# One decoder step on one core: w_ada unsplit on TensorE in four column groups, identity products between its blocks, and DVE operations put at the end of a step

## The chip, the cores and the metric

The kernel runs on one core of a Trainium2 chip. Its engines are TensorE (PE in the rows; its weight loads are PEld), VectorE (DVE), ScalarE (ACT), GpSimd (POOL) and SyncE (SP), whose queue issues the transfers (DMA). The metric is the device time of one execution in microseconds, the median of several runs.

## The reference

One layer over a prompt of 2048 tokens and 8 sampled sequences of 4 tokens, model width 1024, all in float32. Two groups of heads stand side by side: HGRN2 (8 heads, a gated linear recurrence) and mLSTM (4 heads, a matrix memory).

```python
mod = jnp.dot(jax.nn.silu(c), w_ada) + b_ada            # c: one row for the prompt, 8 for the sampled sequences
shift, scale, gate = jnp.split(mod, 3, axis=-1)
h = _rms(x, norm_g) * (1 + scale[:, None]) + shift[:, None]
proj = jnp.dot(h, w_in) + b_in                           # q, f, i(v), z of HGRN2; u, z, o and two gates of mLSTM
o_h, S_new = _hgrn2(qh, logf, vh, S_h, chunk)            # chunkwise; exact per token
y_h = _head_rms(o_h, hgrn_norm_g) * silu(hz)
xc = silu(causal_conv4(mu)); q, k, v = block-diagonal products of xc, xc, mu
h_m, C, n, m = _mlstm(q, k, v, ig, logsigmoid(mf), C, n, m, chunk)
y_m = (_head_rms(sigmoid(mo) * h_m, mnorm_g) + skip * xc) * silu(mz)
out = x + gate[:, None] * jnp.dot(concat(y_h, y_m), w_out)   # then a last RMS norm
```

## The kernel before, in words

**Float32 in pieces.** A large product is made of float32r operands: a tensor is split into a rounded high part (a copy on ACT, line 206) and a low part (a difference on POOL or DVE, line 207), and three products (high-high, low-high, high-low) take the place of one.

**The start.** SyncE issues the loads in program order. `ada_rows` (lines 448 to 470) streams the first 2048 columns of w_ada, 8 MB, as 16 pieces of 128 x 1024, with four in flight. Each is split by ACT and by DVE (every fourth by POOL), and four products of 512 columns per piece, with 42 stationary columns `scs` (silu(c), high and low parts), add into four banks of PSUM. Between the pieces `ada_step` issues small loads and the norm of the first two x tiles. `ada_shift_scale` (lines 472 to 486) brings the rows out, transposes them and forms `msh` (shift) and `msc` ((1 + scale) times norm_g). Then the first unit of w_in is split (`stream_unit(0)`), and `x_modulate` transposes a scaled x tile, applies msc and msh into `hst` and splits the result into `hhi` and `hlo`, the stationary operands of every projection.

**The steady part.** The prompt is worked in four segments (`s`) of 512 tokens. In each segment 48 units of w_in columns follow in a written order (`ORDER`): wide units v and o (256 columns, `proj_tok`, line 563) and narrow units f, q, z, mu, mz (128 columns, `proj_ct`, line 549). In segment 0 units are loaded raw, split, and their parts stored in DRAM (`wdr`); later segments load the parts. A ring of four buffers (tag `w8`) holds the split weights, three buffers (tag `raw`) the raw ones.

**Steps.** After each group of products of a unit, `pump` lets every generator of the list `rec` issue its next piece of work: `hgrn` and `hgrn_out` of a head, `conv`, `mlstm`, `gates`, `bd_prep` (block-diagonal matrices from the small weights, `bd_fill`), statistics of the next x tiles. A generator's yields say how many steps later its next products come, so that TensorE finds them ready between the projection products. Engines work through their instructions in program order. In `hgrn` a chain of states goes from DVE (`U`, line 677) to POOL (`pscale`, line 121) and back, four times a head. `mlstm_out` scales `num` on POOL by a factor `fin` that DVE forms after four ACT squares; three steps later TensorE transposes it (`ph`, line 1324).

**The end.** The output product with w_out (line 1743), from about 1850 us on, is touched by nothing in the change.

## Time and profile before

| | |
|---|---|
| time, median of 3 runs | 2248.98 us (2247.84 to 2250.97) |
| the profiled execution: its own time | 2243.03 us |
| its span, first to last instruction | 2241.2 us |
| PE busy | 2170.0 us, 97% of the span |
| DVE, ACT, POOL busy | 57%, 44%, 19% |
| mean granted TensorE clock | 0.989 |
| transfers | 405.26 MB, mean 181 GB/s |

The busy shares are means over stages with different limits. A busy time of PE counts pipelined products whose ends are modelled, so in what follows the starts of instructions are read rather than their lengths. The granted clock is 1.00 at TensorE's upper level (2.4 GHz) and 0.50 at its lower one (1.2 GHz).

### The profile page before, as it was taken

To read this page: it belongs to the slowest core of one execution; us is meant where nothing else is said; L and a number is where in the kernel's file an instruction comes from. 1 tells how busy PE (TensorE), PEld (TensorE's weight loads), DVE (VectorE), ACT (ScalarE), POOL (GpSimd) and SP (SyncE) were. 2 spreads that over 40 slices of the span, in tenths; PEclk is the share of its full clock that TensorE was granted. 3 is DMA by queue.
4 is the path that set the end of the run, shared out by engine and by line. 5 is a ranking of instruction groups with operands and counts; after the bars stand their busy time and mean duration, and the time that the engine had idled before them with its cause. 6 is when DMAs were issued, how large, how long until landed. Compare 5 with 4: busy or idle time off the path is not lost.

```text
span 2241.2 us, 35168 instructions
## 1 busy us (share of the span) xinstructions
PE 2170.0 (97%) x13594; PEld 1915.1 (85%) x13594; DVE 1268.8 (57%) x2664; ACT 979.1 (44%) x2260; POOL 432.0 (19%) x436
## 2 busy tenths in 40 slices
PE   6999999999999999999999999999999998999998
PEld 3888998787899889899988898888899987888885
DVE  7675657566756574566574555655455675423232
ACT  6445554464443354353444454534444535212121
POOL 3424353341112020212010212110101033000000
PEclk8999999999999999999999999999999999999999
DMA  7676766864546465634465555454555566533330
GB/s 257 214 234 219 262 221 205 302 227 155 189 152 228 167 230 193 217 136 158 179 203 202 189 192 180 162 169 163 146 194 161 174 193 173 165 108 96 93 99 27
DMA packets 225318, 405.26 MB, mean 181 GB/s; under 512 B 24843, under 2 KB 168627, under 8 KB 196470
## 3 DMA queue, kind: packets, MB, share of 16 engines
q1 hardware_dynamic: 225142, 402.92, 54.2%
q8 instruction: 109, 1.79, 0.3%
q14 instruction: 67, 0.55, 0.1%
HBM read 298.43 MB, written 104.44 MB: 180 GB/s over the span
## 4 chain that ended last, share of the span: by engine, by line
PE 68%; DVE 4%; ACT 3%; DMA 1%; issue 1%; POOL 1%; SPq 0%; DVEq 0%; ACTq 0%; POOLq 0%
PE pct L549 27%; PE pout L1743 15%; PE ptok L563 11%; PE p L1151 1%; PE pc L1135 1%; PE pv L1064 1%; PE pp L663 1%; PE pa L639 1%; PE pq L1081 1%; PE po L687 1%; PE po L689 1%; PE psx L1108 1%; ACT st L92 1%; PE p L1135 1%; DMA raw<-in_w_out_dram 1%
## 5 line engine op out<-in xcount | busy, mean ns | idle before, releaser
L549 PE MATMUL pct<-hhi,w 128*128 128x512 f32 (+1 forms) x3200 | 852.0, 354 | 1.2 <-DVE S L697 1.2
L549 PEld LDWEIGHTS pct<-hhi,w 128*128 128x128 f32 x3200 | 552.9, 188 | 74.4 <-issue 3.3
L549 PE MATMUL pct<-hlo,w 128*128 128x512 f32 (+1 forms) x1600 | 560.6, 350 | 0.0
L549 PEld LDWEIGHTS pct<-hlo,w 128*128 128x128 f32 x1600 | 301.0, 188 | 39.2
L563 PE MATMUL ptok<-whi,hhi 128*128 128x256 f32 x1024 | 301.4, 294 | 4.4 <-ACT hhi L92 3.3
L563 PE MATMUL ptok<-whi,hlo 128*128 128x256 f32 x1024 | 291.2, 284 | 0.2 <-DVE hlo L426 0.2
L563 PE MATMUL ptok<-wlo,hhi 128*128 128x256 f32 x1024 | 290.9, 284 | 0.0
L1743 PE MATMUL pout<-wh,y 128*128 128x512 f32 (+1 forms) x792 | 247.2, 391 | 3.0 <-ACT wh L92 3.0
L563 PEld LDWEIGHTS ptok<-whi,hhi 128*128 128x128 f32 x1024 | 197.4, 193 | 7.8 <-ACT hhi L92 3.7
L563 PEld LDWEIGHTS ptok<-wlo,hhi 128*128 128x128 f32 x1024 | 197.6, 193 | 2.3 <-issue 2.2
L563 PEld LDWEIGHTS ptok<-whi,hlo 128*128 128x128 f32 x1024 | 197.3, 193 | 0.9 <-DVE hlo L426 0.9
L1743 PEld LDWEIGHTS pout<-wh,y 128*128 128x128 f32 (+1 forms) x792 | 148.2, 187 | 35.8 <-ACT wh L92 3.5
L1743 PE MATMUL pout<-wl,y 128*128 128x512 f32 (+1 forms) x408 | 159.8, 392 | 1.1 <-POOL wl L1780 0.6
L92 ACT ACTIVATE xo<-oo 128x512 f32<-128x512 f32 (+1 forms) x34 | 21.5, 632 | 249.5 <-DVE oo L1831 249.5
L92 ACT ACTIVATE e<-e 128x512 f32<-128x512 f32 (+1 forms) x160 | 102.0, 638 | 58.9 <-DVE e L1034 54.8
L1826 DVE TENSOR_TENSOR oo<-pout,gate 128x512 f32<-128x512 f32 x32 | 22.0, 687 | 186.3 <-PE pout L1743 185.4
L617 POOL TENSOR_SCALAR tn<-tn,noml,oml 128x512 f32<-128x512 f32 (+1 forms) x32 | 52.6, 1643 | 385.5 <-ACT G L92 384.8
L207 POOL TENSOR_TENSOR w<-raw,w 128x1024 fp32r<-128x1024 f32 x40 | 97.2, 2436 | 113.5 <-ACT w L92 95.1
L121 POOL TENSOR_SCALAR num<-num,fin 128x256 f32<-128x256 f32 x64 | 35.1, 566 | 401.7 <-DVE fin L1313 357.8
L1161 DVE SCALAR_TENSOR_TENSOR Cc<-Cc,dec,pc 128x258 f32<-128x258 f32 x120 | 52.4, 478 | 84.0 <-PE pc L1135 84.0
L1743 PEld LDWEIGHTS pout<-wl,y 128*128 128x128 f32 (+1 forms) x408 | 75.6, 185 | 19.7 <-POOL wl L1780 1.3
L1032 DVE SCALAR_TENSOR_TENSOR xc<-mu,cols,xc 128x512 f32<-128x512 f32 (+1 forms) x120 | 83.7, 698 | 4.2
(403 smaller groups left out, 3792.2 us busy)
## 6 DMA issues: line engine op xcount, KB each, us to landing
w<-wdr SPq DMA_DIRECT2D x120, 1024.0 KB
wdr<-w SPq DMA_DIRECT2D x40, 1024.0 KB
raw<-in_w_in_dram SPq DMA_DIRECT2D x56, 512.0 KB
whi<-wdr SPq DMA_DIRECT2D x24, 1024.0 KB
wlo<-wdr SPq DMA_DIRECT2D x24, 1024.0 KB
raw<-ydr SPq DMA_DIRECT2D x29, 512.0 KB
xt<-in_x_prompt_dram SPq DMA_DIRECT2D x28, 512.0 KB
raw<-in_w_ada_dram SPq DMA_DIRECT2D x16, 512.0 KB
```

The source lines that it names most:

```text
L92: nc.scalar.activation(out, in_, func, bias=bias, scale=scale, **kw)
L121: pool.tensor_scalar(out, in_, sc, 0.0, op0=ALU.mult, op1=ALU.add)
L207: eng.tensor_tensor(lo, raw, hi.bitcast(F32), op=ALU.subtract)
L549: pe.matmul(ps[:, :n], w[:, k, :], h[:, k, t0:t0 + n], start=(i == 0), stop=(i == 3 * KD - 1))
L563: pe.matmul(ps[:, :2 * P], h[:, k, t0:t0 + n], w[:, k, :], start=(i == 0), stop=(i == 3 * KD - 1))
L617: pool.tensor_scalar(tn[:, :W], tn[:, :W], noml[:, h:h + 1], oml[:, h:h + 1], op0=ALU.mult, op1=ALU.add)
L639: pe.matmul(pa[:, t], kt[:, t], qt[:, t])
L663: pe.matmul(pp[:, c * CH:c * CH + CH], ktT[:, c], v[:, c, vc])
L1032: vec.scalar_tensor_tensor(o, src(r), C("cw", 8 * r + k), o, op0=ALU.mult, op1=ALU.add)
L1135: pe.matmul(out[:, :DH + 2], a[:, x], b[y][:, c], start=(q == 0), stop=(q == 2))
L1161: vec.scalar_tensor_tensor(Cc[:, j], Cc[:, j], dec[:, i, c:c + 1], pcs[j][:, :DH + 2], op0=ALU.mult, op1=ALU.add)
L1743: pe.matmul(acc[g][:n if n == CH else 2 * n], a, b[:, 512 * g:512 * g + 512], start=(k == 0 and q == 0), stop=(k == KO - 1 and q == len(mm ...
```

## The change

- **w_ada.** `ada_rows` no longer splits. It loads eight blocks of 128 x 2048 (four in flight, in the ring's buffers) and multiplies them as float32: for each block four products of 512 columns with the same 32 stationary columns `sct` (9 used, the rest zero), each into its own group of 32 rows of one PSUM bank. `ada_shift_scale` becomes one copy, four transposes, two additions and the multiplication by norm_g. The high and low parts `scs` are still made, later (`gate_prep`), for the gate columns.
- **Identity products.** `fill` issues products of the identity with itself into an unread bank: 10 ahead of the first block, 5 behind each block, 3 behind the last, 10 ahead of the first modulation.
- **First unit.** Its first half is split by ACT and POOL, its second by ACT and DVE, with the DVE difference put between the modulation and the split of the first x tile.
- **`late`.** A list of operations that `pump` issues after all generators of the step have issued theirs. Into it go the scan and scaling operations of `hgrn`, the normalisation and the last products of `hgrn_out`, the last product of `conv`, the scaling of `num` and the last products of `mlstm_out`, with their stores.
- **Moved between engines.** The state scaling in `hgrn` goes from POOL to DVE; the fills of `bd_prep` from DVE to POOL.
- **Reordered.** In `mlstm` the splits of a chunk's head; the bias rows of a wide unit are loaded at the end of the wide unit before; the x tiles of the next segment are scaled on POOL a unit, or a step, later than they are loaded.

```diff
...
@@ -440,49 +446,43 @@
     def toks(smp):
         return [(c, c * CH, CH) for c in range(NCH)] + ([(NCH, SEG, NSM)] if smp else [])
-    NB = 1 + NSEQ
-
-    def ada_piece(n):
-        k, b = divmod(n, 2)
-        t = Bt("wada", [P, D]) if n % 2 else raw_tile()
-        sync.dma_start(t, w_ada[k * P:k * P + P, b * D:b * D + D])
+    def fill(junk, n):
+
+        for _ in range(n):
+            pe.matmul(junk[:, :P], ident, ident)
+
+    def ada_load(k):
+        t = ring.tile([P, 2 * D], F32, tag="w8", name="wada", bufs=4)
+        sync.dma_start(t, w_ada[k * P:k * P + P, :2 * D])
         return t
     def ada_rows(step):
-        acc = [ps_tile("pada") if b % 2 else ps_tile("pada") for b in range(4)]
-        raw = {n: ada_piece(n) for n in range(4)}
-        for n in range(2 * KD):
-            k, b = divmod(n, 2)
-            step(n)
-            r = raw.pop(n)
-            t = ring.tile([P, 2, D], F32R, tag="w8", name="wadas", bufs=4)
-            act(t[:, 0], r, AF.Copy)
-            (pool if n % 4 == 3 else vec).tensor_tensor(t[:, 1], r, t[:, 0].bitcast(F32), op=ALU.subtract)
-            for g in range(2):
-                c = slice(512 * g, 512 * g + 512)
-                for y in range(2):
-                    pe.matmul(acc[2 * b + g][:ML], scs[:, k], t[:, y, c], start=(k == 0 and y == 0),
-                              stop=(k == KD - 1 and y == 1))
-            if n + 4 < 2 * KD:
-                raw[n + 4] = ada_piece(n + 4)
+        junk, acc = ps_tile("fill"), ps_tile("pada")
+        fill(junk, 10)
+        w = {k: ada_load(k) for k in range(4)}
+        for k in range(KD):
+            step(k)
+            t = w.pop(k)
+            for q in range(4):
+                pe.matmul(acc[32 * q:32 * q + 32], sct[:, k], t[:, 512 * q:512 * q + 512], start=(k == 0),
+                          stop=(k == KD - 1), skip_group_check=True)
+            fill(junk, 5 if k < KD - 1 else 3)
+            if k + 4 < KD:
+                w[k + 4] = ada_load(k + 4)
         return acc
     def ada_shift_scale(acc):
-        rows = Bt("arows", [NB, D])
-        rows2 = Bt("arows", [NB, D])
-        for b in range(4):
-            dst = (rows, rows2)[b // 2][:, 512 * (b % 2):512 * (b % 2) + 512]
-            act(dst, acc[b][:NB], AF.Copy)
-            vec.tensor_tensor(dst, dst, acc[b][32:32 + NB], op=ALU.add)
-        for r, dst, one in ((rows, msh, 0.0), (rows2, msc, 1.0)):
-            ps = ps_tile("padt")
-            for k in range(KD):
-                pe.transpose(ps[:, k * NB:k * NB + NB], r[:, k * P:k * P + P], ident[:NB, :NB])
-            v = ps[:, :KD * NB].rearrange("p (k b) -> p k b", k=KD)
-            c0 = KD if one else 0
-            vec.scalar_tensor_tensor(dst, v, one, acol[:, c0:c0 + KD, None].to_broadcast([P, KD, NB]),
-                                     op0=ALU.add, op1=ALU.add)
+        r = Bt("arows", [P, 512])
+        vec.tensor_copy(r, acc)
+        ps = ps_tile("padt")
+        for c in range(4):
+            pe.transpose(ps[:, c * P:c * P + P], r[:, c * P:c * P + P], ident)
+        v = ps.rearrange("p (c q b) -> p q c b", c=4, q=4)
+        for x, dst in ((0, msh), (1, msc)):
+            vec.tensor_tensor(dst.rearrange("p (g c) b -> p g c b", g=2), v[:, 2 * x:2 * x + 2, :, :NB],
+                              acol[:, x * KD:x * KD + KD].rearrange("p (g c) -> p g c", g=2)[:, :, :, None]
+                              .to_broadcast([P, 2, 4, NB]), op=ALU.add)
         vec.tensor_tensor(msc, msc, C8("norm_g")[:, :, None].to_broadcast([P, KD, NB]), op=ALU.mult)
     def ada_gate(g, u):
...
@@ -584,6 +585,8 @@
             for g in list(rec):
                 if next(g, "end") == "end":
                     rec.remove(g)
+            while late:
+                late.popleft()()
     def drain(g=None):
         while rec and (g is None or g in rec):
@@ -609,12 +612,16 @@
         G = M("G")
         sigmoid(tn[:, :W], tn[:, :W])
         act(G[:, :W], tn[:, :W], AF.Ln, bias=lb[:, h:h + 1], scale=oml[:, h:h + 1])
-        vec.tensor_tensor_scan(G[:, :W], hmask[:, :W], G[:, :W], 0.0, op0=ALU.mult, op1=ALU.add)
         g4 = G[:, :SEG].rearrange("p (c u t) -> p c u t", u=2, t=CH // 2)
         mid = small("mid", [P, NCH, 1])
-        vec.tensor_copy(mid, g4[:, :, 0, CH // 2 - 1:CH // 2])
-        vec.tensor_tensor(g4[:, :, 0], g4[:, :, 0], mid.to_broadcast([P, NCH, CH // 2]), op=ALU.subtract)
-        pool.tensor_scalar(tn[:, :W], tn[:, :W], noml[:, h:h + 1], oml[:, h:h + 1], op0=ALU.mult, op1=ALU.add)
+
+        def decays():
+            vec.tensor_tensor_scan(G[:, :W], hmask[:, :W], G[:, :W], 0.0, op0=ALU.mult, op1=ALU.add)
+            vec.tensor_copy(mid, g4[:, :, 0, CH // 2 - 1:CH // 2])
+            vec.tensor_tensor(g4[:, :, 0], g4[:, :, 0], mid.to_broadcast([P, NCH, CH // 2]), op=ALU.subtract)
+            pool.tensor_scalar(tn[:, :W], tn[:, :W], noml[:, h:h + 1], oml[:, h:h + 1], op0=ALU.mult, op1=ALU.add)
+
+        late.append(decays)
         yield
         yield
         Ep = M("Ep")
@@ -626,9 +633,13 @@
             act(sm[:, 2 * NCH:], G[:, SEG:].rearrange("p (q t) -> p q t", t=SLEN)[:, :, SLEN - 1], AF.Exp)
         act(G[:, :W], G[:, :W], AF.Exp, scale=-1.0)
         beta = small("beta", [P, NCH])
-        vec.tensor_tensor(beta[:, :NCH - 1], sm[:, 0:NCH - 1], sm[:, NCH + 1:2 * NCH], op=ALU.mult)
-        vec.tensor_tensor(Ep[:, :W], hq[:, :W], Ep[:, :W], op=ALU.mult)
-        vec.tensor_tensor(tn[:, :W], tn[:, :W], G[:, :W], op=ALU.mult)
+
+        def scaled():
+            vec.tensor_tensor(beta[:, :NCH - 1], sm[:, 0:NCH - 1], sm[:, NCH + 1:2 * NCH], op=ALU.mult)
+            vec.tensor_tensor(Ep[:, :W], hq[:, :W], Ep[:, :W], op=ALU.mult)
+            vec.tensor_tensor(tn[:, :W], tn[:, :W], G[:, :W], op=ALU.mult)
+
+        late.append(scaled)
         kt, qt = tn, Ep
         yield
         yield
@@ -675,7 +686,7 @@
             else:
                 u = small("U", [P, P], 1)
                 vec.tensor_tensor(u, R[c], pc, op=ALU.add)
-                pscale(nxt, u, sc)
+                vec.tensor_scalar(nxt, u, sc, None, op0=ALU.mult)
             if c < NCH - 1:
                 R[c + 1] = nxt
         store(sdr[h] if s < NSEG - 1 else hgrn_p[0, 0, h], nxt)
...
@@ -1310,9 +1325,13 @@
                 act(junk[:n], nm[:n, c, :DH], AF.Square, scale=f[:n, 1, c:c + 1], accum=f[:n, 2, c:c + 1])
             act(ss, ss, AF.Ln, scale=1.0 / DH, bias=epsc[:n])
             act(ss, ss, AF.Exp, scale=-0.5)
-            vec.tensor_tensor(kap, ss, rh, op=ALU.mult)
-            for c in range(nch):
-                pscale(nm[:n, c, :DH], nm[:n, c, :DH], f[:n, 3, c:c + 1])
+
+            def scale(nm=nm, n=n, nch=nch, f=f):
+                vec.tensor_tensor(f[:n, 3, :nch], f[:n, 2, :nch], f[:n, 1, :nch], op=ALU.mult)
+                for c in range(nch):
+                    pscale(nm[:n, c, :DH], nm[:n, c, :DH], f[:n, 3, c:c + 1])
+
+            late.append(scale)
         yield
         yield
         yield
...
@@ -1367,10 +1390,16 @@
         units += us
     start.append(len(units))
-    def bias_bc(c0):
-        t = small("bb", [P, 2 * P], 1)
-        sync.dma_start(t, bcast_ap(b_in[0, c0:c0 + 2 * P], P))
-        return t
+    bias = {}
+
+    def bias_load(u):
+
+        while u < len(units) and units[u][1] not in ("v", "mo"):
+            u += 1
+        if u < len(units):
+            c0 = (OI if units[u][1] == "v" else OMO) + 2 * units[u][2] * P
+            bias[u] = small("bb", [P, 2 * P], 1)
+            sync.dma_start(bias[u], bcast_ap(b_in[0, c0:c0 + 2 * P], P))
     KO = 2 * D // P
     KA, NH = 4, 3
...
@@ -1542,7 +1573,7 @@
                 pe.matmul(ps[:, :P], bt[k - 2][:, 2], bt[k - 2][:, 3])
                 if k % 4 == 2:
                     bo = Bt("bo", [P, 4, 2, P])
-                bd_fill(bo[:, (k - 2) % 4, 0], 2, k - 2, vec)
+                bd_fill(bo[:, (k - 2) % 4, 0], 2, k - 2, pool)
                 vec.tensor_copy(bo[:, (k - 2) % 4, 1], ps[:, :P])
                 if k % 4 == 1:
                     store(bdd[:, k - 5:k - 1], bo)
...
@@ -1568,25 +1599,43 @@
         x_rstd(0, c)
         x_scale(0, c, x0[c][0], x0[c][2])
-    def ada_step(n):
-        if n < len(row_loads):
-            sync.dma_start(*row_loads[n])
-        if n in (1, 3):
-            x0.append(x_load(0, len(x0)))
-        if n in (6, 8):
-            x_norm(n // 2 - 3)
-        if n == 13:
+    pre = []
+
+    def ada_step(k):
+        if k < 4:
+            for d in row_loads[4 * k:4 * k + 4]:
+                sync.dma_start(*d)
+        if k == 0:
+            x0.append(x_load(0, 1))
+        if k in (2, 4):
+            x_norm(k // 2 - 1)
+        if k == 3:
+            gate_prep()
+        if k == 4:
+            pre.extend(x_transpose(x0[0][0], CH, g) for g in range(2))
+        if k == 5:
             cols_prep()
+    x0.append(x_load(0, 0))
     acc = ada_rows(ada_step)
-    assert len(row_loads) <= 13
+    assert len(row_loads) <= 16
     load_pieces(1)
     for c in range(2, NCH):
         x0.append(x_load(0, c))
-    pre = [x_transpose(x0[0][0], CH, g) for g in range(2)]
     ada_shift_scale(acc)
-    stream_unit(0)
-    x_modulate(*x0[0], pss=pre, eng=None)
+
+    class Lazy:
+        def tensor_tensor(self, *a, **k):
+            late.append(lambda: vec.tensor_tensor(*a, **k))
+
+    def flush():
+        while late:
+            late.popleft()()
+
+    stream(0)
+    stream(0, eng=Lazy())
+    fill(ps_tile("fill"), 10)
+    x_modulate(*x0[0], pss=pre, eng=None, mid=flush)
     x_norm(2)
     x_modulate(*x0[1], eng=None)
     x_norm(3)
...
@@ -1665,6 +1715,8 @@
         def x_next(c):
             nxt[c] = x_load(s + 1, c)
+
+        def x_now(c):
             x_scale(s + 1, c, nxt[c][0], nxt[c][2])
         def after_last(k_):
@@ -1672,12 +1724,17 @@
                 x_next(k_ + 2)
             if k_ < NCH:
                 x_modulate(*nxt.pop(k_))
+            if k_ + 2 < NCH:
+                x_now(k_ + 2)
         for j in range(per):
             u = base + j
             if j == per - 2 and not last:
                 x_next(0)
                 x_next(1)
+            if j == per - 1 and not last:
+                x_now(0)
+                x_now(1)
             if j == (5 if s == 0 else 1 if last else 2):
                 g = gates(s)
                 next(g)
...
```

## Rows read from the trace of the kernel before

**Rows 1.** The page's line of the span and, from its first section, the line of busy time (us, share of the span, instructions) of each engine.

```profile
span 2241.2 us, 35168 instructions
...
PE 2170.0 (97%) x13594; PEld 1915.1 (85%) x13594; DVE 1268.8 (57%) x2664; ACT 979.1 (44%) x2260; POOL 432.0 (19%) x436
```

**Rows 2.** What TensorE waited for, over the whole span: who waited <- for whom, us in total, times, the longest in us.

```profile
PE pada L465 <- DVE wadas L461: 7.9, 5, 3.4
PE ph L1324 <- POOL num L121: 6.7, 4, 4.2
PE po L689 <- DVE R L674: 4.2, 3, 3.2
PE pb L1542 <- DVE bt L1554: 4.2, 1, 4.2
...
PE pa L639 <- DVE tn L631: 3.6, 5, 1.1
...
PE pxt L397 <- POOL xt L121: 1.8, 1, 1.8
```

**Rows 3.** Busy time by stretches of the start: the stretch in us, its length, busy us and instructions of each engine, granted TensorE clock (1.00 is the upper level), busy share of the DMA engines, GB/s.

```profile
4.00:24.00 20.00, 10.53 (x33) 3.95 (x32) 14.74 (x28) 13.25 (x25) 7.26 (x4) 1.00 1.02 398
24.00:28.00 4.00, 2.98 (x7) 1.30 (x8) 3.57 (x3) 3.91 (x5) 1.34 (x2) 0.66 0.65 206
44.00:60.00 16.00, 13.85 (x88) 13.29 (x88) 10.50 (x26) 14.87 (x38) 9.20 (x5) 0.79 0.82 219
48.00:52.00 4.00, 4.00 (x21) 4.00 (x21) 2.60 (x7) 3.91 (x11) 1.12 (x1) 0.50 0.48 23
```

**Rows 4.** The start in order of time, all engines: start in us, duration in us, engine, line, operation, out<-in, partitions x elements, how many merged, and in brackets the idle time before and what ended it.

```profile
6.28 1.04 ACT L92 ACTIVATE wadas<-raw 128x1024 fp32r<-128x1024 f32 x1
...
32.30 3.28 DVE L461 TENSOR_TENSOR wadas<-wada,wadas 128x1024 fp32r<-128x1024 f32 x1
...
41.42 0.23 DVE L484 SCALAR_TENSOR_TENSOR msh<-padt,acol 128x72 f32<-128x72 f32 x1
41.54 4.65 POOL L207 TENSOR_TENSOR wlo<-raw,whi 128x1024 fp32r<-128x1024 f32 x2 [7.03 <-ACT whi L92]
...
42.16 1.82 DVE L486 TENSOR_TENSOR msc<-msc,cols 128x72 f32<-128x72 f32 x1
...
46.15 0.58 PE L563 MATMUL ptok<-whi,hhi 128*128 128x256 f32 x1 [3.27 <-ACT hhi L92]
...
63.50 0.63 PE L549 MATMUL pct<-hhi,w 128*128 128x512 f32 x2
```

**Rows 5.** TensorE in order of time, columns as in rows 4: two fp32 products of 512 columns (pq), eight of 257 columns into four groups of 32 output rows (p2S), four of 128 columns (pa) and four transposes (pk). An fp32 product leaves two records, a transpose one.

```profile
154.44 1.88 PE L1081 MATMUL pq<-xc,bm 128*128 128x512 f32 x4
...
156.27 0.28 PE L563 MATMUL ptok<-wlo,hhi 128*128 128x256 f32 x1
156.39 0.28 PE L563 MATMUL ptok<-whi,hlo 128*128 128x256 f32 x1
...
785.26 0.42 PE L1248 MATMUL p2S<-raw,qsS 128*32 128x257 f32 x3
...
785.94 0.39 PE L1248 MATMUL p2S<-raw,qsS 128*32 128x257 f32 x3
...
786.27 0.75 PE L1259 MATMUL pcS<-vs,kx 128*128 128x258 f32 x4
...
317.97 1.13 PE L639 MATMUL pa<-Ep,tn 128*128 128x128 f32 x8 [1.13 <-DVE tn L631]
318.94 0.60 PE L642 MATMUL pk<-ident,tn 128*128 128x128 f32 x4
```

**Rows 6.** The stretch of 100 to 130 us as in rows 3, one DVE operation from PSUM as in rows 4, and the block-diagonal fills on DVE and on POOL (line, engine, operation, count: shortest/median/longest ns, first and last start in us).

```profile
100.00:130.00 30.00, 24.80 (x124) 20.86 (x123) 27.28 (x58) 11.65 (x30) 11.10 (x8) 0.89 0.48 123
...
117.76 0.75 DVE L1441 TENSOR_SCALAR sz<-pct,cols 128x512 f32<-128x512 f32 x1
...
L331 DVE TENSOR_TENSOR bt<-bdw,oh x16: 277/282/1957, 73.1 to 154.6; 128x128 f32<-128x128 f32 x16
...
L331 POOL TENSOR_TENSOR bdf<-bdw,oh x8: 388/487/844, 1481.9 to 1840.2; 128x128 f32<-128x128 f32 x8
```

**Rows 7.** What DVE waited for, over the whole span, columns as in rows 2.

```profile
DVE fin L1313 <- ACT fin L92: 55.1, 20, 3.1
DVE U L677 <- POOL R L121: 48.7, 89, 2.6
...
DVE v L1486 <- DMA bb<-in_b_in_dram: 28.9, 9, 5.4
...
DVE hlo L426 <- POOL hhi L424: 17.9, 12, 8.9
```

**Rows 8.** The stretch of 500 to 510 us as in rows 3, and the POOL operation in it that scales an x tile, as in rows 4.

```profile
500.00:510.00 10.00, 8.15 (x57) 7.88 (x56) 2.90 (x7) 3.92 (x8) 3.31 (x4) 0.83 0.72 299
...
504.60 1.12 POOL L121 TENSOR_SCALAR xt<-xt,rstd 128x1024 f32<-128x1024 f32 x1 [16.62 <-DMA xt<-in_x_prompt_dram]
```

**Rows 9.** SyncE's queue waiting for DVE at the bias load, TensorE's weight loads waiting for num (both as in rows 2), and three terms of a convolution on DVE (as in rows 4).

```profile
SPq L1372 <- DVE mo L1486: 59.3, 8, 13.0
...
PEld ph L1324 <- POOL num L121: 9.5, 10, 4.7
...
1537.33 2.32 DVE L1032 SCALAR_TENSOR_TENSOR xc<-mu,cols,xc 128x512 f32<-128x512 f32 x3
```

More of the change, by code (lines that the diff above doesn't have):

```diff
@@ L234, in keep, with split @@
                     sync.dma_start(self.kept[i], x.bitcast(F32))
-        def split(self, j):
+        def split(self, j, eng):
             if self.again:
@@ L240, in split @@
             c = slice(P * j, P * j + P)
-            split(self.raw.pop(j), self.hi[:, :, c], self.lo[:, :, c], pool if self.src is w_in else vec)
+            split(self.raw.pop(j), self.hi[:, :, c], self.lo[:, :, c], eng if self.src is w_in else vec)
     cols = con.tile([P, P], F32, name="cols")
@@ L248, in hymba_step @@
     vec.tensor_copy(acol[:, :96], pt[:, P:P + 96])
+    vec.tensor_scalar(acol[:, KD:2 * KD], acol[:, KD:2 * KD], 1.0, None, op0=ALU.add)
     def C(nm, k):
@@ L574, in hymba_step @@
     stores = deque()
+    late = deque()
     def pump(n=1):
@@ L1137, in mlstm @@
         cur = head(0)
-        ch = None if first else c_split()
         yield
@@ L1391, in alloc, with split @@
             self.hi, self.lo = t[:, 0], t[:, 1]
-        def split(self, j):
-            split(self.raw, self.hi, self.lo)
+        def split(self, j, eng):
+            split(self.raw, self.hi, self.lo, eng)
     units += [(NSEG, "out", k, OutUnit(k)) for k in range(KA)]
@@ L1415, in stream @@
                 unit.alloc()
-            unit.split(j)
+            unit.split(j, eng)
             npiece[0] += 1
@@ L1481, in run_unit @@
             ts = small(kind + "s", [P, 2 * P], 1) if smp else None
-            bb = bias_bc((OI if kind == "v" else OMO) + 2 * n * P)
+            bb = bias.pop(u)
             def evac(ps, c, w):
@@ L1497, in run_unit @@
             pump(steps)
+        if kind in ("v", "mo"):
+            bias_load(u + 1)
         if kind == "q":
```

99 lines of the change are left out of this document (54 added, 45 removed).

## The prediction

> **What bounds the kernel now.** I read the page's first section first: PE is busy for 2170.0 of the span's 2241.2 us [rows 1]. So a time can only fall where PE idles, where its clock is low, or where its work shrinks. The profiled execution took 2243.03 us, 1.8 more than its span; the median of the three runs is 2248.98, 5.95 above it. My sum is made on the profiled execution, and the forecast is that plus 5.95. A difference under 0.2% (4.5 us) is what a measurement of this kernel can hardly tell from none.
>
> Next I read what PE waited for [rows 2]. The largest sum, 7.9 us, is the conditioning (w_ada) stage. The rest are single stalls of at most 4.2 us, most where DVE or POOL delivered late. Then I took the start by stretches [rows 3] and in order of time [rows 4]. The reader is to see two things. The transfers run at 398 GB/s from 4 to 24 us, and then stop being fed: 206 GB/s from 24 to 28. And the conversion of w_ada into pairs on ACT, DVE and POOL ends long after the data: DVE's next-to-last difference runs from 32.30 to 35.58, after all transfers of w_ada, and one more follows. The modulation scale, msc, is ready at 43.98 (42.16 + 1.82), the first product of the first unit starts at 46.15, and that unit (v) gives way to the next at 63.50.
>
> **The change, part by part.**
>
> *w_ada.* All 16 splits go (ACT copies, DVE and POOL differences); PE takes the fp32 blocks directly, four products of 512 columns into four groups of 32 output rows. Their price rests on whether the four groups run side by side. One fp32 product of 512 columns over all output rows costs about 0.85 us: two of them and one small product, of 0.12 us by the spacing of the next, lie between 154.44 and 156.27 [rows 5]. In one file a block would cost 3.4 us. But the sampled heads already issue products to four groups: eight of 257 columns begin at 785.26 and all are out of the way at 786.27, and each set of four takes about 0.45 us [rows 5], a quarter of single file. Scaled to 512 columns that is 0.92 us a block. Bounds 0.9 and 3.4; I take 0.92, since form and type are the same. Five identity products cost 5 x 0.24 = 1.2 us (four took 0.97 [rows 5]), so 2.1 us a block. A block is 1.05 MB, 2.63 us at 398 GB/s. PE keeps up, and the transfer sets the pace.
>
> With four blocks of 1 MB in flight the queue does not run dry: block k+4 is issued after block k's products, with over 2 MB still queued. Ahead of the end of w_ada lie 8.39 MB, two x tiles (1.05) and about 0.1 of small loads: 9.55 MB / 398 GB/s = 24.0 us from 4.0, so 28.0. In the kernel before, the first 0.5 MB, which at this rate is through by 5.5, was taken up by ACT at 6.28 [rows 4]: add 0.8. Last block usable: 28.8. Then products 0.92, the copy out of PSUM 0.75 (as another 128x512 operation of DVE from PSUM [rows 6]), four transposes 0.6 [rows 5], two additions at 0.23 [rows 4] and handing over: 32.2. The multiplication by norm_g follows. Alone it is some 0.2. In the trace it took 1.82 and ended at 43.98 with POOL's first split of w_in (41.54 plus half of 4.65 = 43.87) [rows 4]. The change keeps a split on POOL here. Its raw data land after w_ada, 1.3 us later; with ACT's 1.0 the split runs from about 31.2 to 33.5. So I take msc at 33.7, with 32.4 as its lower bound: 10.3 us before 43.98.
>
> The Trainium skill, SBUF — State Buffer, section "Who interferes with whom", says that a DVE instruction with two SBUF inputs and a GpSimd instruction that reads SBUF exclude each other for the whole instruction. The trace agrees: 1.82 instead of some 0.2 us here. By a reading without that lock msc would come at 32.4 and the forecast be 1.3 lower. The rule also speaks against the second half of the change, below.
>
> From msc to the end of unit v ACT is the limit: 14.87 us busy of 16 [rows 3], with statistics, modulation and splits that the change leaves. The second wlo piece moves to DVE between modulation and hlo: at most 1.2 us there, beside ACT; I add 0.3. So 63.50 - 10.3 + 0.3, a shift of 10.0 us, which is carried to the end because PE is the bound. Bounds: 8 (transfers at 370 GB/s) to 11.6 (no lock).
>
> *Identity products.* They fill PE's gaps. In the trace the clock is at 0.50, the lower of its two levels, from 48 to 52 us [rows 3], behind a wait of 3.27 us of PE that ended at 46.15 [rows 4]. The first tile's 24 products of unit v run in that stretch; at the upper level one comes every 0.12 us [rows 5], so half the clock costs 24 x 0.12 = 2.9 us at most. I count nothing: ACT sets that stretch. If that cover goes, it is a gain.
>
> *DVE operations put behind the others of their step, and scaling from POOL to DVE.* DVE stood behind ACT at the head of its queue for 55.1 us (fin) and behind POOL's R for 48.7 [rows 7]. The last goes: the scaling is now a 128x128 operation of DVE, which I price like a fill on DVE, 0.28 [rows 6], 120 times: 34 us more work against 48.7 of waiting, and DVE is busy for 57% of the span [rows 1]. But `late` only reorders inside one step, and an operation that was already last gains nothing. Of the 3.6 (pa) and 4.2 (po) of PE [rows 2] I count 2; bounds 0 and 7.8.
>
> *Block-diagonal fills from DVE to POOL.* Between 100 and 130 us DVE is busy for 27.28 of 30, PE idles for 5.2 and its clock of 0.89 costs another 3.3 [rows 6]. Per prepared block, three fills of 0.28 leave DVE and cost 0.49 on POOL [rows 6]. I take a third of the 8.5 back: 3. Bounds -2 (rival c) and 8.5.
>
> *Loads and scaling of the next x tiles.* POOL waited 16.62 us for a transfer at the first segment's end, with hhi behind it, and DVE waited for POOL's hhi for up to 8.9 [rows 7, 8]; PE lost 1.8 plus 0.17 x 10 by the clock [rows 2, 8]. With the scaling put after the modulation I count 3; bounds 0 and 4.
>
> *Bias loads* issued a unit ahead: DVE waited 28.9 us for them at v alone [rows 7], no PE wait names them; 0. SP now waits for DVE at each such load; before it did so 8 times for 59.3 us [rows 9], and PE waited for no weights. Against all this I set 2 us for operations that come later than before. Steady part: 2 + 3 + 3 - 2 = 6, bounds -8 and 20.
>
> *Sum.* 2243.0 - 10.0 - 6 = 2227; plus 5.95: **2233 us**.
>
> **Rivals.**
> (a) The four groups run in single file. A block then costs 3.4 + 1.2 = 4.6, eight from 9 us end at about 45, msc comes at 49, 5 later than now; with the steady 6 the time is 2248. Against it: [rows 5]. 3%.
> (b) The other side: deferral starves the transposes of num. The scale factor now stands behind whatever DVE does in that step, such as a convolution (2.32 us for three of its four terms [rows 9], so about 3.1 in all), and POOL and PE wait for it. PE's weight loads already waited for num ten times [rows 9], so there the slack is gone: 10 x 3.1 = 31 us against the 16 gained, 2264. It decides from 1.6 us in each of the ten. For it: one of the two longest stalls of the steady part (4.2) is of this kind [rows 2]. Against it: mostly nothing heavy follows in the step. 5%.
> (c) POOL and DVE shut each other out. 24 fills of 0.49 on POOL are 11.7 us, nine of them (4.4 us) between 100 and 130, where DVE has 2.7 to spare; then this stretch gives nothing, and PE loses 2 more: 2238. The Trainium skill's lock (same section) would do just that; in the trace splits and DVE operations collide so, fills on POOL are not seen beside a loaded DVE. 12%.
> (d) The start is not freed: ACT or the w_in transfer holds the first unit, so that under half of the shift arrives, and `late` gives nothing: 2244. 9%.
> (e) Each of the three steady parts reaches its upper bound, 7.8 + 8.5 + 4 = 20: 2219. For it: DVE's waits [rows 7] are ten times what PE lost by them, so it may run far enough ahead. 11%.
>
> **How the numbers follow.** My forecast (2226 to 2241) has 60%. With (c) inside it and (e) and (d) at the ends, the range is 2218 to 2244. Faster by over 0.2% (below 2244.5): forecast, (c), (e) and half of (d), 0.87. Within: half of (d), (a): 0.08. Slower: 0.05, (b).
>
> **What would show it.** Right: w_ada's last products before 31 us, transfers near 400 GB/s without a gap to 28, four-group products at 0.9 us a block, msc at 32 to 34, unit v over by 54; no POOL R behind DVE U; the PE stall at the first segment's end gone; PE idle past 64 us lower by some 6. Wrong: blocks spaced by more than 2.8 us, v ending after 58, or PE waits for ph, pa and po that grow past 64 us by more than the start gives.

## The result and the profile after

The changed kernel takes 2220.53 us, the median of 4 runs (2218.15 to 2224.13), against 2249.39 (2247.84 to 2250.97) for the kernel before in the same session: a ratio of 0.9873, 95% interval 0.9856 to 0.989, or 28.9 us. The forecast was 2233, in a range of 2218 to 2244.

The profiled execution of after took 2221.07 us, that of before 2243.03. So only 22.0 of the 28.9 us lie between the two profiles. The rest is that the profile of before was of one of its shortest executions and that of after was an ordinary one. I come back to it in the first experiment.

The page of after, the lines that answer to [rows 1]:

```profile
span 2219.3 us, 35329 instructions
...
PE 2165.3 (98%) x13698; PEld 1918.0 (86%) x13698; DVE 1270.5 (57%) x2745; ACT 957.7 (43%) x2240; POOL 385.0 (17%) x336
```

PE's idle time fell from 71.2 us (2241.2 - 2170.0) to 54.0 (2219.3 - 2165.3), and its busy time by 4.7, though it runs 58 identity products more (two records each). A part of the gain is therefore products that ran faster, not products that started sooner: the mean granted clock is 0.993 against 0.989.

What TensorE waited for in after, the largest sums and the rows that answer to [rows 2] (who <- whom, us in total, times, longest):

```profile
PE p2S L1263 <- DMA cs<-in_state_mlstm_C_dram: 4.9, 3, 3.5
PE pb L1573 <- DVE bt L1585: 4.4, 1, 4.4
PE ph L1343 <- POOL num L121: 4.4, 3, 3.8
...
PE po L700 <- DVE R L685: 3.9, 2, 2.6
...
PE pa L650 <- DVE tn L640: 1.7, 3, 0.7
...
PE pxt L401 <- POOL xt L121: 1.5, 1, 1.5
```

The conditioning stage, 7.9 us at the top of [rows 2], is gone from the top of the list. `ph` and `pa` lost about 2 us each, `po` 0.3, `pxt` 0.3, and `pb` did not move. Two waits of before that [rows 2] left out matter below, that for the sampled state `cs`, which grew, and that for `st`:

```profile
PE p2S L1248 <- DMA cs<-in_state_mlstm_C_dram: 2.7, 2, 2.2
...
PE p L1135 <- ACT st L92: 2.2, 4, 1.1
```

The start of after by stretches (columns as in [rows 3]):

```profile
4.00:8.00 4.00, 4.00 (x19) 4.00 (x20) 2.64 (x16) 2.12 (x7) 0.00 (x0) 1.00 0.97 389
24.00:28.00 4.00, 3.62 (x28) 1.74 (x28) 0.29 (x1) 0.00 (x0) 0.00 (x0) 1.00 1.00 403
48.00:52.00 4.00, 3.77 (x30) 3.39 (x29) 3.30 (x9) 2.37 (x6) 2.47 (x1) 1.00 1.04 277
```

The transfers stay near 400 GB/s to 28 us, where before had 206, and at 48 to 52 the clock is 1.00 where it was 0.50. The same start in order of time (columns as in [rows 4]):

```profile
9.25 1.09 PE L468 MATMUL pada<-wada,sct 128*32 128x512 f32 x8 [0.57 <-DMA wada<-in_w_ada_dram]
10.27 1.38 PE L452 MATMUL fill<-ident 128*128 128x128 f32 x10
...
29.22 1.07 PE L468 MATMUL pada<-wada,sct 128*32 128x512 f32 x8
30.36 0.69 DVE L477 COPY arows<-pada 128x512 f32<-128x512 f32 x1 [5.35 <-PE pada L468]
...
32.04 2.35 POOL L207 TENSOR_TENSOR wlo<-raw,whi 128x1024 fp32r<-128x1024 f32 x1 [10.71 <-ACT whi L92]
32.27 2.22 DVE L486 TENSOR_TENSOR msc<-msc,cols 128x72 f32<-128x72 f32 x1
...
53.99 0.64 PE L549 MATMUL pct<-hhi,w 128*128 128x512 f32 x2
```

A block's four products (two records each) take 10.27 - 9.25 = 1.02 us: they run side by side. The last block is through at about 30.2, msc is ready at 32.27 + 2.22 = 34.49, and unit v gives way at 53.99, 9.5 us sooner than the 63.50 of [rows 4].

Stage by stage, from the starts of the same products in both traces: 9.5 us up to the end of unit v; 0.8 in the rest of segment 0 (430.6 us before, 429.8 after); 4.5 between the segments, from the third transposed x tile to the first gate product (46.6, 42.1); 4.1 from there to the first output product (1314.0, 1309.9); 2.9 in the output stage (386.4, 383.5). That makes 21.8, the difference of the spans (21.9) but for rounding. Each is the difference of two single executions; the output stage varies by about 1 us among executions of kernels that agree in it.

All that lies behind unit v, before and then after (columns as in [rows 3]):

```profile
63.50:2241.20 2177.70, 2127.69 (x13386) 1887.04 (x13384) 1223.30 (x2571) 938.00 (x2184) 406.96 (x418) 0.99 0.54 178
```

```profile
53.99:2219.30 2165.31, 2121.85 (x13386) 1884.89 (x13384) 1247.17 (x2667) 934.53 (x2184) 372.44 (x322) 0.99 0.55 180
```

For the same 13386 records TensorE idles 6.5 us less (50.0, 43.5) and is busy 5.8 us less.

### The profile page after: what moved, and what is told of

Same layout as the page of the kernel before. It is cut to its first block, busy times and chain, and to the rows that moved or that the text cites. A ratio compares the mean times of both kernels' runs of the same rounds, so it can differ in the third digit from the quotient of the medians.

```text
span 2219.3 us, 35329 instructions
## 1 busy us (share of the span) xinstructions
PE 2165.3 (98%) x13698; PEld 1918.0 (86%) x13698; DVE 1270.5 (57%) x2745; ACT 957.7 (43%) x2240; POOL 385.0 (17%) x336
## 4 chain that ended last, share of the span: by engine, by line
PE 79%; DVE 8%; DMA 4%; ACT 4%; issue 3%; POOL 2%; SPq 1%; POOLq 0%; ACTq 0%; DVEq 0%
PE pct L549 31%; PE pout L1800 15%; PE ptok L563 15%; PE pc L1152 2%; PE p L1167 2%; PE pv L1081 1%; PE po L700 1%; PE po L698 1%; PE pq L1098 1%; PE psx L1125 1%; PE pa L650 1%; DMA cs<-in_state_mlstm_C_dram 1%; PE pp L674 1%; PE p L1152 1%; ACT st L92 1%
## 5 line engine op out<-in xcount | busy, mean ns | idle before, releaser
L92 ACT ACTIVATE num<-p,zc 128x257 f32<-128x257 f32 x60 | 28.3, 471 | 148.7 <-PE p L1167 148.6
```

Source lines behind the costliest of these rows:

```text
L92: nc.scalar.activation(out, in_, func, bias=bias, scale=scale, **kw)
```

## Experiments

All kernels compute the whole layer. "Whole change" is the changed kernel.

**The kernel before, again.**

> The kernel before, unchanged, timed against itself. The change moved the median by 28.9 us but the profiled executions by 22.0 (2243.03 to 2221.07). Theory A (the profiled execution of before was by chance a short one): ratio 1.000, and the new profiled execution lies near the median, within 2 us of it. Theory B (taking a profile shortens this kernel by some 6 us): the profiled execution again lies 5 to 7 us under the median.

Measured: 2246.95 us (2243.21 to 2250.28, 11 runs), ratio 0.9997 [0.9988, 1.0006]. The profiled execution took 2243.82, 3.1 under the median, which is neither the 2 us of theory A nor the 5 to 7 of theory B. What decides is the row of all profiles: those of the thirteen kernels run after the prediction lie between 3.1 under and 2.6 above their own medians, that of after 0.5 above. So the 5.95 us, which I carried over, were mostly a low draw of before's profile and no property that another kernel must share. The granted clock explains the spread only in part: in these 11 executions the four at a mean of 0.990 are the shortest (2243.21 to 2244.64), but of the 21 of the same kernel beside them one at 0.990 took 2249.21 and one at 0.985 took 2247.99.

**The start alone:** w_ada unsplit, identity products, first split on POOL and DVE; the steady part as before.

```diff
-            act(t[:, 0], r, AF.Copy)
-            (pool if n % 4 == 3 else vec).tensor_tensor(t[:, 1], r, t[:, 0].bitcast(F32), op=ALU.subtract)
...
+            for q in range(4):
+                pe.matmul(acc[32 * q:32 * q + 32], sct[:, k], t[:, 512 * q:512 * q + 512], start=(k == 0),
+                          stop=(k == KD - 1), skip_group_check=True)
```

> Only the start of the change: w_ada unsplit in four column groups, identity products, first unit split on POOL and DVE. My sum gives 10.0 us (the trace of the changed kernel 9.5 at the end of the first unit): ratio 0.9955 to 0.996. Rival (the start also frees something later, or the clock kept up carries on): 15 us or more, ratio under 0.9935. Rival (the start is absorbed later): under 5 us, ratio over 0.998.

Measured: 2238.02 us (2236.34 to 2239.41), ratio 0.996 [0.9946, 0.9973], 9.4 less than the 2247.42 of its session. Unit v ends at 54.7. The start carries through to the end alone.

**`late` alone.**

```diff
+            while late:
+                late.popleft()()
...
-        vec.tensor_tensor(Ep[:, :W], hq[:, :W], Ep[:, :W], op=ALU.mult)
+        late.append(scaled)
```

> Only the operations put at the end of a step (late), nothing else. My step: 2 us less (bounds 0 and 7.8), ratio 0.9965 to 1.000. Rival (late carries the steady part of 12 us that the milestones show past the first unit): ratio under 0.996. Rival b of the prediction (the factor of num comes too late): ratio over 1.002.

Measured: 2238.39 us (2236.24 to 2239.68), ratio 0.9958 [0.9944, 0.9971]: 9.0 less, against a term of 2. The execution that was profiled (2239.68) was its slowest, and shows 3.4 against the profile of before, so the 9.0 rests on the medians.

**The handover alone:** x tiles scaled later, bias rows loaded earlier.

```diff
+            if k_ + 2 < NCH:
+                x_now(k_ + 2)
...
-            bb = bias_bc((OI if kind == "v" else OMO) + 2 * n * P)
+            bb = bias.pop(u)
```

> Only the loads and the scaling of the next x tiles at the end of a segment, and the bias loads a unit ahead. My step: 3 us less (bounds 0 and 4); by the milestones of the two traces the end of the first segment gives 4.6 and each later one 1 to 2: ratio 0.9965 to 0.9985. Rival (the gain at the handover comes from late or from the mlstm order, not from these): ratio 0.9995 to 1.001.

Measured: 2245.9 us (2243.36 to 2250.79, 11 runs), ratio 1.0 [0.9991, 1.0009]: the median is 1.5 less, the ratio can't be told from none, against a term of 3.

These parts make 18.4 of some 28, so the rest had to lie in parts not tried, or in company. The next runs take one part at a time out of the whole change.

**The whole change, again.**

> The changed kernel itself, so that the kernels with one part left out have their base on the same chip. Single executions of the kernel before range from 2243 to 2251 us with granted clocks of 0.986 to 0.991, those of the changed kernel so far from 2218 to 2224 with 0.992 to 0.993. Theory (the profiled execution of before was one of its short ones, and the offset of 5.95 us that the prediction added does not carry over): median 2219 to 2222 with profile and median within 3 us of each other; ratio 0.987 to 0.989.

Measured: 2221.17 us (2218.03 to 2221.59) against 2246.51, ratio 0.9884 [0.9869, 0.9899], 25.3 less. It is the yardstick of the kernels that follow, and their diffs are against the changed kernel.

**Without the moves between engines:** the scaling of U on POOL, the fills of `bd_prep` on DVE, as before.

```diff
-                vec.tensor_scalar(nxt, u, sc, None, op0=ALU.mult)
+                pscale(nxt, u, sc)
...
-                bd_fill(t[:, 0], 0, k, pool)
+                bd_fill(t[:, 0], 0, k, vec)
```

> The whole change, but the state scaling of hgrn stays on POOL and the block-diagonal fills on DVE. The parts timed alone so far give 9.4 (start), 9.0 (late) and 1.5 (loads, handover) of some 27. Theory D (the engine moves give a good part of the missing 7): 3 to 7 us slower than the whole change, ratio 0.989 to 0.991. My step (2 + 3 us at most, and by the milestones of the traces nearly nothing up to 490 us): 0 to 3 us slower. Rival c (POOL and DVE exclude each other): faster than the whole change by 1 to 4.

Measured: 2219.23 us, ratio 0.9881 [0.9866, 0.9896]. Together the moves bring nothing; each by itself was not tried. The wait of `pb` is 4.2 us in before and 4.4 in after and here, so it does not hang on who makes the fills. DVE and POOL around it in after (columns as in [rows 4]):

```profile
102.78 2.57 POOL L207 TENSOR_TENSOR w<-raw,w 128x1024 fp32r<-128x1024 f32 x1
103.14 2.79 DVE L970 TENSOR_TENSOR gm<-gf,gm 4x544 f32<-4x544 f32 x1
105.31 1.96 POOL L335 TENSOR_TENSOR bo<-bdw,oh 128x128 f32<-128x128 f32 x1
```

and without the moves:

```profile
101.47 2.37 POOL L207 TENSOR_TENSOR w<-raw,w 128x1024 fp32r<-128x1024 f32 x1
101.50 2.38 DVE L950 COPY i<-gi 4x32 f32<-4x32 f32 x1
...
106.04 0.71 DVE L970 TENSOR_TENSOR gm<-gf,gm 4x544 f32<-4x544 f32 x1
...
112.71 0.29 DVE L335 TENSOR_TENSOR bo<-bdw,oh 128x128 f32<-128x128 f32 x1
...
113.12 0.41 DVE L1585 COPY bt<-pb 128x256 f32<-128x256 f32 x1
```

In both kernels one DVE operation is held up beside POOL's split of a w_in piece, only not the same one: in after `gm`, 2.79 us instead of 0.71, here the copy to `i`, 2.38 us where after has 0.39. So the long `gm` is not the doing of the fills. A fill on POOL that begins beside `gm` takes 1.96 us, where their median is 0.40; a DVE operation that a fill holds up does not show in this stretch. And the fills hardly stand in front of `pb`: from 99.7 to the copy at 113.12 us, which `pb` waits for, DVE goes from one operation to the next, most of them of `gates`, and one of them is a fill, of 0.29 us. The loss of 2 us that rival (c) expected is as large as this comparison can tell from none, and the last two kernels below, which differ by the same moves, lie the other way round (2219.66 us with them, 2220.44 without).

**Without `late`:** all its operations back in place, the rest of the change kept.

```diff
-        late.append(scaled)
+        vec.tensor_tensor(Ep[:, :W], hq[:, :W], Ep[:, :W], op=ALU.mult)
+        vec.tensor_tensor(tn[:, :W], tn[:, :W], G[:, :W], op=ALU.mult)
```

> The whole change, but every late operation stands where it stood before. Alone, late gave 9.0 us in the median, and 3.2 in the one profiled execution, almost all of them after 1850 us. Theory E (late's gain stands by itself): 7 to 10 us slower than the whole change, ratio 0.991 to 0.992. Rival (its gain overlaps with the engine moves and the handover): 0 to 5 us slower. My step (2 us): 2 slower.

Measured: 2233.96 us (2231.38 to 2236.0), ratio 0.9945 [0.9931, 0.9958]. In company `late` is worth 12.8. Where it comes from shows, at one place, in DVE's order of time. Without `late` (columns as in [rows 4]):

```profile
451.97 0.74 DVE L1446 TENSOR_SCALAR sz<-pct,cols 128x512 f32<-128x512 f32 x1
452.63 0.71 DVE L1332 TENSOR_TENSOR szm<-szm,e 128x544 f32<-128x544 f32 x1
453.26 0.90 DVE L1335 SCALAR_TENSOR_TENSOR xs<-ph,cols,xs 128x512 f32<-128x512 f32 x2
454.19 1.98 DVE L1337 TENSOR_TENSOR xs<-xs,szm 128x544 f32<-128x544 f32 x1
456.09 0.74 DVE L645 COPY_PREDICATED atm<-causal,pa 128x512 f32<-128x512 int32 x1
...
463.06 0.35 DVE L675 TENSOR_SCALAR R<-pp,beta 128x128 f32<-128x128 f32 x1
```

TensorE behind it, and the stretch around it (columns as in [rows 3]):

```profile
463.47 0.69 PE L690 MATMUL po<-R,Ep 128*128 128x128 f32 x2 [2.77 <-DVE R L675]
```

```profile
444.00:493.00 49.00, 45.56 (x256) 39.50 (x255) 39.91 (x65) 26.53 (x60) 19.94 (x11) 0.97 0.54 187
```

With `late` (the whole change, again), DVE and then the stretch:

```profile
447.64 0.74 DVE L1470 TENSOR_SCALAR sz<-pct,cols 128x512 f32<-128x512 f32 x1
448.30 0.74 DVE L655 COPY_PREDICATED atm<-causal,pa 128x512 f32<-128x512 int32 x1
...
455.89 0.74 DVE L1470 TENSOR_SCALAR sz<-pct,cols 128x512 f32<-128x512 f32 x1
456.55 0.33 DVE L685 TENSOR_SCALAR R<-pp,beta 128x128 f32<-128x128 f32 x1
```

```profile
441.00:485.00 44.00, 43.94 (x254) 37.90 (x253) 39.03 (x63) 24.86 (x56) 19.74 (x11) 1.00 0.60 204
```

Without `late`, `szm` and `xs`, whose results only go to a store, stand between the evacuation `sz` and `atm`, then again before `R`: from the end of `sz` to `atm` 3.4 us pass instead of none, and TensorE waits 2.77 us for R. The clock of the stretch is 0.97 instead of 1.00. With `late`, PE is busy for 43.94 of 44 us.

Two things more stand in the traces. Without `late` the other edits make segment 0 longer than it was before (437.7 us from the end of unit v to the third x tile, against 430.6), so by these traces a part of the 12.8 makes good what they cost there; `late` alone shortens this way by 3.8 us, to 426.8. And the output stage, which I had called untouched by the change, is shorter with it: 383.4 to 384.2 us in the nine traces of kernels with `late`, 385.5 to 386.4 in the five without. Which of its operations does that was not tried.

**Without identity products.**

```diff
-        fill(junk, 10)
...
-            fill(junk, 5 if k < KD - 1 else 3)
...
-    fill(ps_tile("fill"), 10)
```

> The whole change without any identity product. My step: nothing on the sum, since ACT sets the stretch after msc; unit v ends at 54 as with them, and the granted clock of 32 to 44 us falls to 0.5 in places. Rival (the clock they hold up is worth its time): unit v ends 2 to 4 us later, ratio 0.001 to 0.002 above the whole change. Second rival (they stand in the way of the last block and the transposes): msc 0.5 to 1 us earlier.

Measured: 2218.86 us (2213.14 to 2222.9), ratio 0.9872 [0.9855, 0.989]: they are worth nothing in time. Without them (the products of the first and of the fourth block, then stretches as in [rows 3]):

```profile
8.69 1.93 PE L467 MATMUL pada<-wada,sct 128*32 128x512 f32 x8 [4.55 <-DVE rstd L378]
...
16.14 1.07 PE L467 MATMUL pada<-wada,sct 128*32 128x512 f32 x8 [0.86 <-DMA wada<-in_w_ada_dram]
```

```profile
8.00:12.00 4.00, 2.85 (x16) 0.43 (x16) 1.01 (x6) 0.50 (x2) 1.12 (x1) 1.00 1.01 422
...
36.00:40.00 4.00, 3.02 (x11) 2.58 (x12) 3.85 (x9) 3.74 (x12) 0.48 (x1) 0.50 0.96 180
```

The first block, behind 4.55 us in which TensorE stood, takes 1.93 us, the fourth 1.07; both are less than the 2.63 of a transfer. The granted clock of that stretch reads 1.00, so the rows don't say what slowed the first. At 36 to 40 us, where the whole change had 0.75 when run again and 1.00 in the profile of after, the clock is at 0.50, the lower level; but ACT is busy for 3.74 of 4 us and sets the pace. Unit v ends at 54.3, as in the whole change, again (54.3).

**Without the handover edits.**

```diff
-            if j == per - 1 and not last:
-                x_now(0)
-                x_now(1)
...
-            bb = bias.pop(u)
+            bb = bias_bc((OI if kind == "v" else OMO) + 2 * n * P)
```

> The whole change without the later scaling of x tiles and without the early bias loads. Alone these gave 1.5 us, inside the noise. Theory F (they pay only with the rest, as the milestones say: in the trace of the whole change the end of the first segment gains 4.6 us, of the kernel with late alone 0): 3 to 6 us slower than the whole change, ratio 0.990 to 0.991. Rival (they are worth nothing anywhere): 0 to 1.5 us slower, ratio 0.988 to 0.989.

Measured: 2218.4 us (2215.37 to 2224.27), ratio 0.9883 [0.9866, 0.99]. Worth nothing that can be told, as alone. By the traces, one execution of each kernel, this nothing is a sum. The stretch between the segments, without the handover edits:

```profile
476.25:522.49 46.24, 41.42 (x298) 38.37 (x296) 25.94 (x63) 22.07 (x51) 6.48 (x10) 0.96 0.57 211
...
341.00:391.00 50.00, 47.38 (x371) 45.92 (x370) 33.36 (x82) 30.75 (x76) 17.42 (x8) 0.97 0.66 220
391.00:441.00 50.00, 47.62 (x248) 35.97 (x248) 32.75 (x81) 27.17 (x57) 21.16 (x15) 1.00 0.87 299
```

and in after:

```profile
483.77:525.84 42.07, 39.28 (x297) 36.78 (x296) 25.34 (x64) 22.06 (x51) 6.54 (x10) 1.00 0.55 201
...
341.00:391.00 50.00, 47.39 (x360) 46.37 (x360) 33.67 (x82) 27.90 (x68) 15.51 (x8) 0.93 0.68 227
391.00:441.00 50.00, 45.17 (x240) 34.16 (x239) 32.41 (x85) 22.63 (x54) 17.12 (x12) 0.97 0.86 292
```

The edits shorten the stretch between the segments from 46.2 to 42.1 us for the same products, 4.2 where I had forecast 3 (alone 2.4, from 46.6 to 44.3). The wait that the forecast rested on, `pxt` for the scaled x tile, is not what went. It stays in after (1.5 us, as listed above). Without the edits TensorE has another wait in this stretch, which after has not:

```profile
496.17 0.38 PE L563 MATMUL ptok<-whi,hhi 128*128 128x256 f32 x1 [1.97 <-DVE y L896]
```

With the edits TensorE idles 2.0 us less there, since that wait is gone and the others even out, and is busy 2.1 us less at the higher clock (39.28 for 41.42).

But with them TensorE idles longer and has a lower clock between 341 and 441 us (there after waits 3.5 us in one piece for the sampled state's transfer `cs`), and it comes to this stretch 7.5 us later (483.77 against 476.25). The profiled execution without the edits, 2215.37, was the shortest of its kernel, so the loss may look larger here than it is; the medians say that gain and loss are about even. That the edits delay `cs` is not shown: kernels without them wait for it too (2.7 us in before, 4.0 with the start alone). Which of them costs the time ahead was not tried; alone they cost none there (430.9 us from unit v to the third x tile, 430.6 before).

**Without the new order in `mlstm`.**

```diff
+            vec.tensor_tensor(dm[:, t], ps[:, :CH], dm[:, t], op=ALU.mult)
+            st = small("st", [P, 2, CH], 2, F32R)
+            act(st[:, 0], dm[:, t], AF.Copy)
+            vec.tensor_tensor(st[:, 1], dm[:, t], st[:, 0].bitcast(F32), op=ALU.subtract)
             xw = small("xw", [P, 2, 2 * P], 1, F32R)
...
-            vec.tensor_tensor(dm[:, t], ps[:, :CH], dm[:, t], op=ALU.mult)
...
-            st = small("st", [P, 2, CH], 2, F32R)
-            act(st[:, 0], dm[:, t], AF.Copy)
...
```

> The whole change with the order of the chunk's head in mlstm as before. The prediction gave it nothing: TensorE waited 2.2 us for st and 0.6 for qs before. Expected 0 to 2 us slower, ratio 0.988 to 0.989. Rival (it is the missing part of the gain): 3 to 7 us slower.

Measured: 2228.08 us (2225.35 to 2230.7), ratio 0.9912 [0.9898, 0.9926]. The order is worth 6 to 7 us (6 by the ratios, 7 by the medians), which no term of my sum had. Its waits and the stretch between the segments:

```profile
PE p L1152 <- ACT st L92: 3.1, 4, 1.3
PE p L1168 <- DVE qs L1141: 0.6, 4, 0.2
```

```profile
485.57:529.88 44.31, 41.33 (x297) 38.48 (x296) 25.66 (x63) 22.28 (x51) 6.51 (x10) 0.96 0.50 182
```

In after, `p` waits for `st` once, 1.3 us. So 1.8 + 0.6 = 2.4 us are waits. In this stretch another 2.05 us are products at a lower clock: TensorE is busy for 41.33 us instead of 39.28 with the same 297 records. Both traces have the same stall of 1.3 us on `st` there, and yet the clock fell only in one, so that the order causes this fall is not shown. About half of the 9.3 us between these two profiles lies in segments 1 to 3: from the first gate product to the first output product this kernel takes 1314.7 us, after 1309.9, with TensorE idle for 12.0 us against 7.9. All eight traces with the new order have 1306.9 to 1312.5 us there, all six without it 1314.0 to 1318.4.

**The scale factor from PSUM.** The sum for msc is written back to PSUM, so that the multiplication has one input in SBUF. The sum for msh now stands behind it.

```diff
-        vec.tensor_tensor(msc, msc, C8("norm_g")[:, :, None].to_broadcast([P, KD, NB]), op=ALU.mult)
...
+        vs = v[:, 2:4, :, :NB]
+        vec.tensor_tensor(vs, vs, cols8(acol[:, KD:2 * KD]), op=ALU.add)
+        vec.tensor_tensor(msc.rearrange("p (g c) b -> p g c b", g=2), vs, cols8(C8("norm_g")), op=ALU.mult)
...
```

> The whole change, but the sum for msc is written back to PSUM and the multiplication by norm_g reads it there, so that this operation of DVE has one operand in SBUF and not two. Theory (DVE waits for the end of POOL's split because both read SBUF): the operation takes 0.2 to 0.3 us beside the split, msc comes at 32.5 to 32.8 where it came at 34.5, and unit v ends 1.5 to 2 us earlier; in the time 1 to 2 us less. Rival (the 2.2 us come from something else, such as the load of norm_g): the operation still takes 2 us or more and ends with the split.

Measured: 2219.66 us (2218.22 to 2221.53), ratio 0.9883 [0.9867, 0.9898]. The place in order of time:

```profile
32.10 2.36 POOL L207 TENSOR_TENSOR wlo<-raw,whi 128x1024 fp32r<-128x1024 f32 x1 [11.04 <-ACT whi L92]
32.27 0.23 DVE L487 TENSOR_TENSOR msc<-padt,cols 128x72 f32<-128x72 f32 x1
...
53.01 0.63 PE L551 MATMUL pct<-hhi,w 128*128 128x512 f32 x2
```

The operation takes 0.23 us instead of 2.22 beside the same POOL split, msc is ready 2 us sooner, and unit v ends at 53.01 instead of 54.3 or 54.0. The Trainium skill, SBUF — State Buffer, section "Who interferes with whom", says that a DVE instruction with at most one SBUF input, outside the modes that use two ports, does not contend with GpSimd: the pair of traces agrees. The 1.0 to 1.3 us gained there are too few to be seen in the time.

**Both together:** the scale factor from PSUM, and no moves between engines.

> The whole change with msc from PSUM and without the engine moves (state scaling on POOL, fills on DVE as before). The engine moves cost 2 us in the median and 3 in the profiled execution; msc from PSUM should give 1 to 2. Theory: 2216 to 2219 us, ratio 0.986 to 0.988. Rival (the two differences were noise): as the whole change, 0.988 to 0.989.

Measured: 2220.44 us (2218.94 to 2220.93), ratio 0.9882 [0.9866, 0.9898]. No version clearly beats the whole change.

## Why the prediction was right, and what in it was mis-sized

The direction, the start and the range held. My own forecast of 2226 to 2241 us did not: the time lies 5.5 us under it, and it is the bound that rival (e) set which holds it in the range. The 6 us of the steady part came out as 12.4 between the two profiles: 6.5 of idle time, close to the 6 that I had named as a sign, and 5.8 of products that ran faster, which I had in no term. Part by part the 6 did not hold, as the list shows; that the idle time came out near it is luck. The miss is 12.5 us (2233 - 2220.5), and it has two parts of about the same size: the profiled execution came 5.9 under the 2227 of the sum, and the offset added to it, 5.95, was -0.5.

- **w_ada: right.** The products were forecast at 0.92 us a block and 28.8 + 0.92 = 29.7 for the last; they took 1.02 and ended at 30.2. msc was forecast at 33.7 and came at 34.49; unit v at 53.5, and 53.99. The shift was 10.0 by the sum, 9.5 in the trace and 9.4 in the run of the start alone. The lock of DVE and POOL cost 2.0 us (2.22 against 0.23), as taken from [rows 4]; of the 1.3 that I set on its absence, 1.0 to 1.3 arrived at unit v. Rivals (a) and (d) fall by these rows.
- **Identity products: right at nothing**, for the reason given (ACT sets that stretch), and the run without them shows it.
- **`late`: mis-sized.** I counted 2 of the 7.8 us that [rows 2] had for `pa` and `po`, since an operation that is last in its step gains nothing. It was worth 9.0 alone and 12.8 in company, more than my upper bound. The step that failed is that only what is moved, and only where it was not yet last in its step, can gain. I looked at operations that were *moved* and asked what they gained. In the stretch shown the gain is with those that stayed: evacuations, `atm` and `R`, which now stand ahead of bulk work. And I priced a stall by its length only: each one that goes can also spare a stretch at a lower clock (0.97 in the stretch shown against 1.00).
- **Fills on POOL: wrong.** 3 us were counted; nothing came. The step that failed is that fills are what loads DVE ahead of the stall: the 4.2 us wait of `pb` stayed (4.4) with the fills on either engine, and in front of the copy that it waits for there is one fill of 0.29 us, in before as well (at 121.99 us). Of rival (c) the outcome came, that this stretch gives nothing. Its mechanism shows between DVE and POOL's splits, in both kernels; that fills on POOL hold DVE up is not shown.
- **Scaling on DVE: the price was right** (0.28 forecast, 0.29 the median of 88, the longest 1.79, beside a split of POOL), and in the run without both moves its worth can't be told apart from that of the fills.
- **Handover: right in size at its place, by another wait, and wrong in the sum.** The 3 us come between the segments (4.2), and are lost elsewhere. The step that failed is the stall: `pxt`, which I had said would be gone, waits 1.5 us where it waited 1.8, and what went is a wait for `y` and time at the lower clock. The 2 us set aside for operations that come later than before were too few: by these two profiles 7.5 us go ahead of that stretch. That fits segment 0 past unit v being only 0.8 us shorter than before, although `late` is worth about 8 us in the same stretch in company (429.8 us from unit v's end to the third x tile with it, 437.7 without).
- **Order in `mlstm`: missed.** I had it in no term, and [rows 2] as I chose them left out its wait (2.2 us in four pieces). 6 to 7 us.
- **Rival (b) did not happen:** the wait of `ph` for `num` fell from 6.7 to 4.4 us. **Rival (e)**, 2219, came nearest in time by another way: of its three parts, one passed its bound and two gave nothing. The 2244 of rival (d) stands for some 1 us of the shift arriving; with half of it the sum would have been 2240 (2233 + 5 + 2).

Taken out or put in one at a time, start (9.4), `late` (9.0 to 12.8) and the order in `mlstm` (6 to 7) make 24 to 29, against 25.3 and 28.9 measured for the whole. As the first was only timed alone and the last only in company, this is a comparison of sizes and no proof that they add up. Effects of 2 us and less are not settled: the executions of one kernel differ by more.

## What to carry to other kernels

In an engine's in-order queue ask of every operation who waits for it next; work that only feeds a store belongs behind the work that the bounding engine waits for, even if the engine as a whole is half idle. Here the gain (9.0 to 12.8 us) was larger than the 7.8 us of stalls that the profile listed for two of its waits. Before moving work off a loaded engine, look what stands in its queue in front of the operation that is waited for: here it was one fill of 0.29 us. Before adding an offset from one profiled execution to a median, look how far that execution lies from the others of its own kernel. And where an edit gives nothing in time, compare stage by stage: a gain in one place and a loss in another call for another repair than an edit without effect.

## What was not expected of the hardware

A 4x544 DVE operation with two tensors in took 2789 ns beside POOL's split of a 128x1024 piece (2.57 us) and 714 ns with no POOL operation beside it; a 128x128 fill on POOL that began beside it took 1.96 us, where the median of these fills is 0.40. TensorE's clock followed equal stalls differently: after a wait of 1.3 us for the same operand between the segments, the mean granted clock of that stretch was 1.00 in one kernel and 0.96 in another, and TensorE's busy time for the same 297 records differed by 2.05 us; with the handover edits alone two such waits of 1.4 us left it at 1.00. Over whole executions of the unchanged kernel, 32 in one session, the mean granted clock lay between 0.985 and 0.991, and the times between 2243.21 and 2251.29 us.
